# Scans of a gated DeltaNet block: side work queued behind the chain by edges, convolutions as a list of steps, the next head's preparation in 22 parts

## The chip, the cores and the metric

The kernel runs on one NeuronCore of a Trainium2 chip. A core has five engines with a queue each, which run side by side and wait for one another at semaphores: TensorE (PE; its weight loads are listed as PEld), VectorE (DVE), ScalarE (ACT), GpSimd (POOL) and SyncE (SP), which issues the DMAs here. The metric is the device time of one execution in microseconds; the time before is the median of three runs.

## The reference

One layer of a backbone over 512 latent tokens and 256 context tokens, width 2048, float32. A modulated RMS norm gives h (latents) and hc (context); one input projection feeds two groups of heads, and one output projection joins them.

```python
h = rms_norm(x, norm_w[l]) * (1.0 + scale) + shift
hc = rms_norm(ctx, norm_w[l]) * (1.0 + scale_c) + shift_c
...
qkv = jax.nn.silu(centred_conv(qkv, conv_w)).astype(jnp.float32)
...
def step(s, inp):
    q_i, k_i, u_i, w_i, g_i, intra_i = inp
    v_new = u_i - jnp.einsum('bhcd,bhde->bhce', w_i, s)
    o_i = (jnp.einsum('bhcd,bhde->bhce', q_i * jnp.exp(g_i)[..., None], s)
           + jnp.einsum('bhij,bhje->bhie', intra_i, v_new))
    g_last = g_i[..., -1:]
    s = (s * jnp.exp(g_last)[..., None]
         + jnp.einsum('bhcd,bhce->bhde', k_i * jnp.exp(g_last - g_i)[..., None], v_new))
    return s, o_i
```

Group A (8 heads of 128) is a gated delta rule in chunks of 64 tokens, one scan forward and one backward, over context and then latents, with a depthwise convolution of 5 taps and a SiLU on q, k and v ahead of it. Every chunk needs the inverse of a triangular 64x64 matrix. Group B (8 query heads, 2 key heads) is attention with per-head norms and rotary positions. Both are multiplied by SiLU gates.

## The kernel before, in words

All large matmuls are done in three passes of split numbers: a weight piece (512 rows by 128 columns, 256 KB) is loaded into wraw, cast on ScalarE into whi (L129), and VectorE subtracts to give wlo (L130); each has three buffers. `proj_steps` (L154) makes the 48 matmuls of a projection tile against h (512 columns, tile names kl, ql, vl, kvl, qal, zal) and, for k, v and the attention's keys and values, the same against hc (256 columns, kx, vx, kvx), from four pieces, and yields the columns of each step. It asks for a piece at the piece's first matmul.

Stages: an opening with modulation and the projections of head 0; a stretch of gates and preparation of head 0; eight scans, one a head; attention; the output projection and the final norm. The order on TensorE is the program's, by hand, up to the end of attention. On the other engines a planner orders the instructions at build time by priority (program order, moved up by `tc.high_priority`) and by when it reckons them ready; in attention ScalarE, VectorE and GpSimd are by hand too.

`gdn_scan` (L824) runs both directions of a head at once, in 12 steps. A step is a chain over engines: the state times the keys on TensorE (ks, L852 to L857), r on VectorE (L866, two halves), the triangular inverse UU times r on TensorE (ts, L875), two scaled copies vs (L879) and vn (L882) on ScalarE, the update on TensorE (L886), the new state st on VectorE (L892; L890 in a head's first step). Off the chain, GpSimd scales the old state into sd (L864, listed at L240), needed by st; ScalarE copies the state's part of the output from ks into oq (L871); TensorE adds the output of the chunk (L895). After ks, ts and the update the generator yields F1, F2 or F3 columns: 35 slots a head. In each slot the main loop (from L1169) does three things: `pull(n)` takes so many columns of the feed; if the slot is in PREP_AT, one part of the next head's preparation is done; in slot 6 the previous head's output is written.

The feed (`feeding`, L1098) is one long list of projection tiles: keys and values of attention, q0, v of head 1, then k, q and v of heads 2 to 7, with attention's tiles between and behind. At the end of a tile `take` (L195) copies it from PSUM into one of three buffers craw, and `gdn_post_k`, `gdn_post_q` or `gdn_post_v` queue at once a whole convolution (`conv`, L204): a scaled copy on ScalarE (L217), four taps on VectorE for the latents and four for the context (L221), a tanh on ScalarE (L224, L225), and two or four SiLU products on VectorE (L237).

`gdn_prep` (L621) makes a head's preparation in 11 parts, at slots 0, 2, 4, 6, 8, 15, 18, 27, 29, 31 and 33 of the scan before: transposed keys with sums of squares (t1 L640, t2 L646, t3 L653; copies and squares on ScalarE), the decay matrix gr (L681 to L686), the products of keys and queries (L693 to L713), transposes NT (L718), a transfer through DRAM (L728, L731), a substitution of 14 rounds on VectorE (tm, NE, L738 and L740), a transfer back (L744, L758), values (L751), and four stages of small matmuls (L771 to L813) up to UU (L821).

Of the kernel before, what the change touches and what calls it, by code (L numbers as in the profile page):

```python
# [68 lines left out]
def build(tc, a):  # L69
# [80 lines left out]
    def proj_tile(col, nm, pl, pc=None):  # L150
        for _ in proj_steps(col, nm, pl, pc):
            pass

    def proj_steps(col, nm, pl, pc=None):  # L154


        for kq in range(4):
            src = w_in[kq * 512:(kq + 1) * 512, col:col + 128].rearrange("(k p) c -> p k c", p=128)
            hi, lo = wpiece(src, f"{nm}_{kq}", 128, V)
            passes = [(kq * 4 + k4, n, lw, rt) for k4 in range(4)  # L160
                      for n, (lw, rt) in enumerate(hpass(kq * 4 + k4, hi[:, k4], lo[:, k4]))]

            def one(out, m, k, n, lw, rt):
                T.matmul(out, lhsT=lw, rhs=rt[m], start=k == 0 and n == 0, stop=k == KT - 1 and n == 2,  # L164
                         skip_group_check=True)

            if pc is not None and kq == 0:
                for out, m, n_ in ((pl, 0, SEQ), (pc, 1, CTX)):
                    for x in passes:
                        one(out, m, *x)  # L170
                        yield n_
                continue
            for x in passes:
                one(pl, 0, *x)
                if pc is not None:
                    one(pc, 1, *x)
                yield SEQ if pc is None else SEQ + CTX
# [17 lines left out]
    def take(pl, pc, raw=None, eng=None):  # L195

        raw = next_craw() if raw is None else raw
# [6 lines left out]
    def conv(t, nm, raw, ctx):  # L204
# [5 lines left out]
        acc = cvp.tile([128, 770], F32, tag="cacc", bufs=CA_BUFS, name=f"cacc_{nm}")  # L210
        acc = acc[:, :n]
# [4 lines left out]
        e = raw[:, 2:]  # L216
        S.activation(acc, raw[:, 0:n], AF.Copy, scale=w(0))  # L217
        for i0, m in ((off, SEQ), (0, CTX))[:2 if ctx else 1]:
            for j in range(1, 5):
                x = acc[:, i0:i0 + m]  # L220
                V.scalar_tensor_tensor(out=x, in0=raw[:, i0 + j:i0 + j + m], scalar=w(j), in1=x,  # L221
                                       op0=ALU.mult, op1=ALU.add)
        if ctx:
            S.activation(e[:, :CTX], acc[:, :CTX], AF.Tanh)  # L224
        S.activation(e[:, off:off + SEQ], acc[:, off:], AF.Tanh)  # L225
        return acc, e, off
# [349 lines left out]
    def next_craw():  # L576

        ncraw[0] += 1
        return craw[ncraw[0] % 3]
# [12 lines left out]

    def gdn_post_k(h, raw):
        kq = kq_of(h)
        kc = kcs[h] = qkp.tile([128, 2, 2, 64], F32, tag="kc", bufs=2, name=f"kc{h}")
        acc, e, off = conv(8 + h, f"k{h}", raw, True)
        x, y = [t[:, off:off + SEQ].rearrange("p (c t) -> p c t", t=64) for t in (acc, e)]
        silu(V, kq[:, 0:4, 0:64], x[:, 0:4], y[:, 0:4])
        silu(V, kq[:, 4:8, 64:128], x[:, 4:8], y[:, 4:8])
        x, y = [t[:, 0:CTX].rearrange("p (c t) -> p c t", t=64) for t in (acc, e)]  # L600
        silu(V, kc[:, :, 0], x[:, 0:2], y[:, 0:2])
        silu(V, kc[:, :, 1], x[:, 2:4][:, ::-1], y[:, 2:4][:, ::-1])

    def gdn_post_q(h, raw):
        kq = kq_of(h)
        acc, e, off = conv(h, f"q{h}", raw, False)
        x, y = [t[:, :SEQ].rearrange("p (c t) -> p c t", t=64) for t in (acc, e)]
        silu(V, kq[:, 0:4, 64:128], x[:, 0:4], y[:, 0:4])
        silu(V, kq[:, 4:8, 0:64], x[:, 4:8], y[:, 4:8])

    def gdn_post_v(h, raw):
        vv = vvs[h] = qkp.tile([128, 6, 2, 64], F32, tag="vv", bufs=1, name=f"vv{h}")
        acc, e, off = conv(16 + h, f"v{h}", raw, True)
        for p0_, n, o in ((2, 4, off), (0, 2, 0)):
            x, y = [t[:, o:o + n * 128].rearrange("p (c t) -> p c t", t=64) for t in (acc, e)]
            silu(V, vv[:, p0_:p0_ + n, 0], x[:, 0:n], y[:, 0:n])
            silu(V, vv[:, p0_:p0_ + n, 1], x[:, n:2 * n][:, ::-1], y[:, n:2 * n][:, ::-1])
# [3 lines left out]
    def gdn_prep(h):  # L621
# [3 lines left out]
        kq, kc, vv = kqs[h], kcs[h], vvs[h]  # L625
# [24 lines left out]
        yield  # L650
        t3 = gtile([128, 2, 128], f"t3{nm}")
# [4 lines left out]
        for p in range(2):  # L656
            S.activation(jk, t3[:, p], AF.Square, accum_out=ss[:, 8 + p:9 + p])

# [21 lines left out]

        V.tensor_tensor(out=gr, in0=gr, in1=gsc["gcum"][:, col].unsqueeze(2).to_broadcast([128, 12, 64]),  # L681
                        op=ALU.subtract)
        for v in range(2):
            V.tensor_tensor(out=gr[:, v * 6:v * 6 + 6], in0=gr[:, v * 6:v * 6 + 6],
                            in1=masks[v].unsqueeze(1).to_broadcast([128, 6, 64]), op=ALU.min)
        S.activation(gr, gr, AF.Exp)  # L686

# [13 lines left out]
        AT = gr  # L701
        V.tensor_tensor(out=gr, in0=gr, in1=cc[:, 1].unsqueeze(2).to_broadcast([128, 12, 64]), op=ALU.mult)
        for v in range(2):
# [10 lines left out]
        for half in range(2):  # L714
            vb = 1 - half
            for blk in range(2):
                b = half * 64 + blk * 32
                V.transpose(out=NT[b:b + 32, :, blk * 32:blk * 32 + 32],  # L718
                            in_=AT[b:b + 32, vb * 6:vb * 6 + 6, blk * 32:blk * 32 + 32])
# [12 lines left out]
        V.memset(NE.rearrange("w j i -> w (j i)")[:, 0:256:17], 1.0)  # L732
        tm = gp.tile([96, 64], F32, tag="tm", bufs=1, name=f"tm{nm}")
        with tc.high_priority(offset=1500):
            for m in range(14, 0, -1):
                n = 15 - m
                tv = tm[:, :m * n].rearrange("w (j i) -> w j i", i=n)
                V.tensor_tensor(out=tv, in0=NE[:, 0:m, m:m + 1].to_broadcast([96, m, n]),  # L738
                                in1=NE[:, m:m + 1, m + 1:].to_broadcast([96, m, n]), op=ALU.mult)
                V.tensor_tensor(out=NE[:, 0:m, m + 1:], in0=NE[:, 0:m, m + 1:], in1=tv, op=ALU.add)  # L740
        nd2 = nd2s[h % 2]
        for s in range(2):
            ds_ = slice(16 * s, 16 * s + 16)
            SY.dma_start(nd2[:, ds_, ds_], NE[48 * s:48 * s + 48])  # L744

        vtok = gp.tile([128, 6, 128], F32, tag="vtok", bufs=2, name=f"vtok{nm}")
        for p0_, n in ((0, 2), (2, 4)):
            yield
            tv_ = (btile if n == 2 else gtile)([128, n, 128], f"tv{nm}_{p0_}")
            for p in range(n):  # L750
                T.transpose(out=tv_[:, p], in_=vv[:, p0_ + p].rearrange("c s t -> c (s t)"), identity=ident)  # L751
            for p in range(n):
                S.activation(vtok[:, p0_ + p], tv_[:, p], AF.Copy, scale=vin[:, p0_ + p:p0_ + p + 1])

        DD = gp.tile([128, 12, 32], F32, tag="DD", bufs=1, name=f"DD{nm}")
        DT = gp.tile([128, 12, 32], F32, tag="DT", bufs=1, name=f"DT{nm}")
        for bi in range(4):
            SY.dma_start(DD[bi * 32:bi * 32 + 32], nd2[bi * 12:bi * 12 + 12].rearrange("w j i -> j w i"))  # L758

# [63 lines left out]

    def gdn_scan(h):  # L824
# [11 lines left out]
        for si, (v, p) in enumerate(steps):  # L836
# [10 lines left out]
            else:  # L847
# [11 lines left out]
                with first_of_all():  # L859
# [5 lines left out]
                    for rows, d in halves:  # L865
                        V.scalar_tensor_tensor(out=r[rows], in0=ks[rows, d], scalar=gsc["negeg"][rows, gcol:gcol + 1],  # L866
                                               in1=vtok[rows, p], op0=ALU.mult, op1=ALU.add)
                if lat:
                    with tc.high_priority(offset=1000):
                        for (rows, _), d in zip(halves, (db, dt_)):  # L870
                            S.activation(oq[rows, v, p - 2], ks[rows, d], AF.Copy,  # L871
                                         scale=gsc["egsw"][rows, gcol:gcol + 1])
# [3 lines left out]
            with first_of_all():  # L876
                if not last:
                    vs = gp2.tile([128, 128], F32, tag="vs", bufs=1, name=f"vs{nm}_{si}")
                    S.activation(vs, ts[:, 2], AF.Copy, scale=cc[:, 2, w:w + 1])  # L879
                if lat:  # L880
                    vn = gp2.tile([128, 128], F32, tag="vn", bufs=1, name=f"vn{nm}_{si}")
                    S.activation(vn, ts[:, 2], AF.Copy, scale=cc[:, 0, w:w + 1])  # L882
            yield F2
            if not last:
# [3 lines left out]
                with first_of_all():  # L888
                    if si == 0:
                        V.tensor_copy(sn, ts[:, 0:2])  # L890
                    else:
                        V.tensor_tensor(out=sn, in0=sd, in1=ts[:, 0:2], op=ALU.add)  # L892
# [134 lines left out]
    PREP_AT = (0, 2, 4, 6, 8, 15, 18, 27, 29, 31, 33)  # L1027
# [12 lines left out]
    gdn_post_v(0, raws[2])  # L1040
    gp = es_g.enter_context(tc.tile_pool(name="gp", bufs=1, reuse_waits="tile"))
# [14 lines left out]
    def feed_k(h):  # L1056
# [3 lines left out]
        gdn_post_k(h, take(pl, pc))  # L1060

    def feed_q(h):
        pl = PP.tile([128, SEQ], F32, tag="pl", name=f"ql{h}")
        yield from proj_steps(COL_Q + h * 128, f"q{h}", pl)
        gdn_post_q(h, take(pl, None))

    def feed_v(h):
# [3 lines left out]
        gdn_post_v(h, take(pl, pc))  # L1071
# [77 lines left out]
    for n in (3000, 5500, 5500, 4000, 14000):  # L1149
        pull(n)  # L1150
        next(prep, None)
    gdn_post_k(1, raws[3])
    pull(9000)
# [4 lines left out]
    gdn_post_q(1, raws[4])  # L1158
    es_x.close()
# [7 lines left out]
    run(prep, 5000, 24000, 5000, 7000, 6000)  # L1167
    tail = None
    for h in range(NH):  # L1169
# [3 lines left out]
        if h + 1 < NH:  # L1173
            prep, prep_at = gdn_prep(h + 1), PREP_AT
        else:
# [4 lines left out]
            prep, prep_at = attn_prep(), (*range(1, 28, 2), 33)  # L1180
        slot = 0
        for n in scan:
            if n is None:
                break
            pull(n)
            if slot in prep_at:
                next(prep, None)
            if slot == 6 and tail is not None:
                next(tail, None)
            slot += 1  # L1190
        for _ in prep:
# [427 lines left out]
```

## Time and profile before

| | us |
|---|---|
| time, median of 3 runs (1294.81 to 1297.11) | 1296.88 |
| the profiled execution | 1292.93 |
| its span, first to last instruction | 1291.1 |
| first scan's first ts to attention's first work, about 240 to 858 | 618 |
| attention, about 858 to 1103 | 245 |
| output projection and norm, 1103 to the end | 188 |

The profile lists busy time by engine, the time in stretches, waits by who waited for whom, and groups of instructions by line. A row of a timeline has the start in us from the span's start, the duration, engine and line, the operation, the tile written and the tiles read; a bracket gives the idle time before it and what ended it. A row of waits has the total in us, the number of waits and the longest. Ends of matmuls are modelled, so two matmuls in a row are drawn overlapping.

### The profile page before, as it was taken

How to read it: one execution, taken by the hardware profiler on the slowest of the kernel's cores; microseconds unless marked ns; L12 is line 12 of the kernel's file. 1: busy time of each engine (PE TensorE's matmuls, PEld its weight loads, DVE VectorE, ACT ScalarE, POOL GpSimd, SP SyncE). 2: the span in 40 equal slices, each digit the busy share in tenths (PEclk: the TensorE clock that was granted, in tenths of full speed). 3: DMA queues.
4: the chain of work that ended last, by engine and by line, in shares of the span. 5: the costliest groups of instructions: out<-in, count | busy, mean ns of one | idle time of the engine just before them, and what ended most of it. 6: DMA issues, size and time to landing. Idle time of an engine off the chain costs nothing. (4 is left out here: it accounts for less than half of the span.)

```text
span 1291.1 us, 24373 instructions
## 1 busy us (share of the span) xinstructions
PE 1241.8 (96%) x9242; PEld 1015.1 (79%) x9242; DVE 849.4 (66%) x1905; ACT 580.7 (45%) x1452; POOL 142.7 (11%) x206
## 2 busy tenths in 40 slices
PE   6899999999999999999999999999999999999997
PEld 4566688878788888888888787777888888788886
DVE  5444586686876769676786646546998997555333
ACT  5222363444545454454644444444455544434211
POOL 1323100111111111111211111100000000000000
PEclk9899999999999999999999999999999999999999
DMA  9999424232222312322232445347445353576302
GB/s 355 319 334 346 134 67 106 55 75 56 67 68 75 72 51 71 76 62 65 62 72 63 104 93 150 102 132 255 136 139 156 109 144 97 174 236 195 90 33 98
DMA packets 227288, 164.53 MB, mean 127 GB/s; under 512 B 62242, under 2 KB 198523, under 8 KB 226147
## 3 DMA queue, kind: packets, MB, share of 16 engines
q1 hardware_dynamic: 226874, 162.87, 43.5%
q8 instruction: 73, 1.20, 0.4%
q14 instruction: 44, 0.36, 0.1%
q10 hardware_dynamic: 297, 0.11, 0.0%
HBM read 148.85 MB, written 14.08 MB: 126 GB/s over the span
## 5 line engine op out<-in xcount | busy, mean ns | idle before, releaser
L240 POOL TENSOR_TENSOR sdh<-sth,egl 128x256 f32<-128x256 f32 x80 | 56.8, 711 | 447.9 <-DVE sth L892 345.3
L871 ACT ACTIVATE oqh<-ksh,egsw 64x128 f32<-64x128 f32 x128 | 46.4, 362 | 93.2 <-DVE rh L866 86.9
L866 DVE SCALAR_TENSOR_TENSOR rh<-ksh,negeg,vtokh 64x128 f32<-64x128 f32 x176 | 61.2, 348 | 31.0 <-PE ksh L854 24.4
L146 PE MATMUL po<-whi_wo,mh 128*128 128x512 f32 x192 | 76.2, 397 | 0.0
L148 PE MATMUL po<-whi_wo,ml 128*128 128x512 f32 x192 | 76.0, 396 | 0.0
L147 PE MATMUL po<-wlo_wo,mh 128*128 128x512 f32 x192 | 76.0, 396 | 0.0
L1358 PE MATMUL zl<-hhL,whi_z 128*128 128x512 f32 x176 | 71.4, 405 | 0.0
L1358 PE MATMUL zl<-hL,whi_z 128*128 128x512 f32 x176 | 69.8, 397 | 0.0
L1358 PE MATMUL zl<-hhL,wlo_z 128*128 128x512 f32 x176 | 69.3, 394 | 0.0
L130 DVE TENSOR_TENSOR wlo_wo<-wraw_wo,whi_wo 128x512 fp32r<-128x512 f32 x48 | 33.1, 690 | 51.5 <-ACT whi_wo L129 51.3
L886 PE MATMUL tsh<-vsh,ktok 128*128 128x128 f32 x352 | 56.6, 283 | 6.9 <-ACT vnh L882 3.5
L886 PEld LDWEIGHTS tsh<-vsh,ktok 128*128 128x128 f32 x352 | 47.3, 190 | 16.2 <-ACT vnh L882 8.1
L129 ACT CAST whi_wo<-wraw_wo 128x512 fp32r<-128x512 f32 x48 | 29.7, 620 | 62.3 <-PE po L148 52.1
L892 DVE TENSOR_TENSOR sth<-sdh,tsh 128x256 f32<-128x256 f32 x80 | 33.6, 420 | 27.4 <-PE tsh L886 19.2
L879 ACT ACTIVATE vsh<-tsh,cch 128x128 f32<-128x128 f32 x88 | 32.2, 366 | 38.8 <-PE tsh L875 37.5
L950 ACT CAST pth<-pt 128x512 fp32r<-128x512 f32 x48 | 26.5, 586 | 44.3 <-PE pt L1287 44.3
L164 PE MATMUL vl<-hhL,whi_v 128*128 128x512 f32 x112 | 46.3, 413 | 0.0
L164 PE MATMUL vl<-hhL,wlo_v 128*128 128x512 f32 x112 | 46.2, 413 | 0.0
L164 PE MATMUL vl<-hL,whi_v 128*128 128x512 f32 x112 | 45.8, 409 | 0.0
L1406 DVE SCALAR_TENSOR_TENSOR gacc<-graw,scol,gacc 128x512 f32<-128x512 f32 x60 | 44.9, 748 | 1.1
L146 PEld LDWEIGHTS po<-whi_wo,mh 128*128 128x128 f32 x192 | 36.1, 188 | 9.5 <-ACT ze L1312 0.8
L148 PEld LDWEIGHTS po<-whi_wo,ml 128*128 128x128 f32 x192 | 36.2, 188 | 8.8
(545 smaller groups left out, 3894.5 us busy)
## 6 DMA issues: line engine op xcount, KB each, us to landing
wada<-in_w_ada SPq DMA_DIRECT2D x64, 512.0 KB, 8.4
graw<-in_w_ada SPq DMA_DIRECT2D x64, 256.0 KB, 3.2
wraw_wo<-in_w_out SPq DMA_DIRECT2D x48, 256.0 KB, 3.1
wraw_z<-in_w_in SPq DMA_DIRECT2D x44, 256.0 KB, 3.0
wraw_v<-in_w_in SPq DMA_DIRECT2D x28, 256.0 KB, 2.9
wraw_k<-in_w_in SPq DMA_DIRECT2D x24, 256.0 KB, 2.8
wraw_q<-in_w_in SPq DMA_DIRECT2D x24, 256.0 KB, 2.8
xs<-in_x SPq DMA_DIRECT2D x4, 1024.0 KB, 5.2
```

The costliest lines, as they stand in the source:

```text
L130: (lo_eng or G).tensor_tensor(out=lo, in0=raw, in1=hi, op=ALU.subtract)
L146: T.matmul(out, lhsT=lh, rhs=rh, start=start, stop=False, skip_group_check=True)
L147: T.matmul(out, lhsT=lh, rhs=rl, start=False, stop=False, skip_group_check=True)
L148: T.matmul(out, lhsT=ll, rhs=rh, start=False, stop=stop, skip_group_check=True)
L164: T.matmul(out, lhsT=lw, rhs=rt[m], start=k == 0 and n == 0, stop=k == KT - 1 and n == 2, skip_group_check=True)
L240: eng.tensor_tensor(out=out, in0=x, in1=y, op=ALU.mult)
L866: V.scalar_tensor_tensor(out=r[rows], in0=ks[rows, d], scalar=gsc["negeg"][rows, gcol:gcol + 1], in1=vtok[rows, p], op0=ALU.mult, op1=ALU.add)
L871: S.activation(oq[rows, v, p - 2], ks[rows, d], AF.Copy, scale=gsc["egsw"][rows, gcol:gcol + 1])
L886: T.matmul(ts[:, d], lhsT=ktok[:, p, half], rhs=vs, start=True, stop=True, skip_group_check=True)
L892: V.tensor_tensor(out=sn, in0=sd, in1=ts[:, 0:2], op=ALU.add)
L1358: T.matmul(pl, lhsT=lw, rhs=rt, start=k == 0 and m == 0, stop=k == KT - 1 and m == 2, skip_group_check=True)
L1406: V.scalar_tensor_tensor(out=acc, in0=raw, scalar=scol[:, k:k + 1], in1=acc, op0=ALU.mult, op1=ALU.add)
```

## The change

Five things, all about order.

1. The scan keeps its latest chain instruction on VectorE (r, st) and on ScalarE (vs, vn) in `behind`. What a slot queues is traced inside `tc.issue_after` of these: each of its instructions on VectorE or ScalarE gets an edge that keeps it behind the chain's.
2. The copies oq go from ahead of ts to behind vn, with such an edge.
3. A convolution becomes a list of steps in a queue, `jobs`, each with its engine ("A" or "D") and a price. `step_jobs` does some of them at the end of a slot: steps of one kind only, VectorE's as long as the slot's budget CAP (1.0, 1.6 or 1.9 us) less what pieces and preparation spent of it lasts, ScalarE's not in the slots after ks. `finish` does all that must be done by then.
4. The preparation has 22 parts, with a price for each in PREP_AT; the rounds of the substitution, queued in slot 8 before, stand in five parts in slots 16 to 21.
5. A piece is loaded 4608 columns of matmuls ahead of its use, by a list (`plan`), instead of at its first matmul.

The instructions are the same in kind and number, and the feed has the same order.

```diff
+    def load_ahead():
+
+        if not plan:
+            return
+        col, nm, kq = plan.popleft()
+        src = w_in[kq * 512:(kq + 1) * 512, col:col + 128].rearrange("(k p) c -> p k c", p=128)
+        made[col, kq] = wpiece(src, f"{nm}_{kq}", 128, V)
+        spent[0] += 0.7
...
+            for ms, n_ in work:
+                if left > AHEAD >= left - n_:
+                    load_ahead()
+                left -= n_
+                for out, m, x in ms:
+                    one(out, m, *x)
+                yield n_
...
+        jobs.append(("A", 0, tag, first))
         for i0, m in ((off, SEQ), (0, CTX))[:2 if ctx else 1]:
             for j in range(1, 5):
...
+                jobs.append(("D", 0.75 if m == SEQ else 0.48, tag, lambda i0=i0, m=m, j=j: tap(i0, m, j)))
+        jobs.append(("A", 0, tag, tanh))
+        for f in last(accs, e, off):
+            jobs.append(("D", 0.42, tag, f))
+
+    def step_jobs(budget, act):
+
+        kind = None
+        while jobs and (kind is None or kind == jobs[0][0]) and (budget > 0 if jobs[0][0] == "D" else act):
+            kind, cost, _, fn = jobs.popleft()
+            fn()
+            budget -= cost
...
-                if lat:
-                    with tc.high_priority(offset=1000):
-                        for (rows, _), d in zip(halves, (db, dt_)):
-                            S.activation(oq[rows, v, p - 2], ks[rows, d], AF.Copy,
-                                         scale=gsc["egsw"][rows, gcol:gcol + 1])
...
+            if lat:
+                with tc.high_priority(offset=1000), tc.issue_after(behind["ACT"].ins):
+                    for (rows, _), d in zip(halves, (db, dt_)):
+                        S.activation(oq[rows, v, p - 2], ks[rows, d], AF.Copy,
+                                     scale=gsc["egsw"][rows, gcol:gcol + 1])
             yield F2
...
-    PREP_AT = (0, 2, 4, 6, 8, 15, 18, 27, 29, 31, 33)
+    PREP_AT = {0: 0, 3: 0, 4: 1.0, 5: 1.1, 6: 0, 7: 1.6, 8: 1.7, 9: 1.0, 10: 0.9, 11: 2.1, 15: 0, 16: 1.3, 17: 1.3,
+               18: 0, 19: 1.3, 20: 1.3, 21: 0.9, 26: 0.6, 27: 0.6, 29: 1.2, 31: 0.3, 33: 1.5}
+    LATE_AT = dict.fromkeys((*range(1, 28, 2), 33), 1.5)
+    CAP = (1.0, 1.6, 1.9)
...
-            pull(n)
-            if slot in prep_at:
-                next(prep, None)
-            if slot == 6 and tail is not None:
-                next(tail, None)
+            spent[0] = prep_at.get(slot, 0)
+            with ExitStack() as order:
+                for x in behind.values():
+                    order.enter_context(tc.issue_after(x.ins))
+                pull(n)
+                if slot in prep_at:
+                    next(prep, None)
+                if slot == 6 and tail is not None:
+                    next(tail, None)
+                step_jobs(CAP[slot % 3] - spent[0], slot % 3 < 2)
             slot += 1
```

More of the change, by code (lines that the diff above doesn't have):

```diff
@@ L1 @@
+from collections import deque
 from contextlib import ExitStack
@@ L165, in one @@
                          skip_group_check=True)
+            left = 12 * (SEQ if pc is None else SEQ + CTX)
             if pc is not None and kq == 0:
[L168 to L177, printed above, removed]
+                work = [(((out, m, x),), n_) for out, m, n_ in ((pl, 0, SEQ), (pc, 1, CTX)) for x in passes]
+            elif pc is not None:
+                work = [(((pl, 0, x), (pc, 1, x)), SEQ + CTX) for x in passes]
+            else:
+                work = [(((pl, 0, x),), SEQ) for x in passes]
+            for ms, n_ in work:
+                if left > AHEAD >= left - n_:
+                    load_ahead()
+                left -= n_
+                for out, m, x in ms:
+                    one(out, m, *x)
+                yield n_
     es_g = ExitStack()
@@ L202, in take, with conv @@
         return raw
-    def conv(t, nm, raw, ctx):
+    jobs = deque()
+    def conv(t, nm, tag, raw, ctx, last):
         n = SEQ + (CTX + 2 if ctx else 0)
@@ L209, in conv, with first, tap, tanh @@
             raw = raw[:, CTX + 2:]
-        acc = cvp.tile([128, 770], F32, tag="cacc", bufs=CA_BUFS, name=f"cacc_{nm}")
-        acc = acc[:, :n]
+        e = raw[:, 2:]
+        accs = []
         def w(j):
             return cvT[:, j * 24 + t:j * 24 + t + 1]
-        e = raw[:, 2:]
-        S.activation(acc, raw[:, 0:n], AF.Copy, scale=w(0))
+        def first():
+            accs.append(cvp.tile([128, 770], F32, tag="cacc", bufs=CA_BUFS, name=f"cacc_{nm}")[:, :n])
+            S.activation(accs[0], raw[:, 0:n], AF.Copy, scale=w(0))
+        def tap(i0, m, j):
+            x = accs[0][:, i0:i0 + m]
+            V.scalar_tensor_tensor(out=x, in0=raw[:, i0 + j:i0 + j + m], scalar=w(j), in1=x,
+                                   op0=ALU.mult, op1=ALU.add)
+        def tanh():
+            if ctx:
+                S.activation(e[:, :CTX], accs[0][:, :CTX], AF.Tanh)
+            S.activation(e[:, off:off + SEQ], accs[0][:, off:], AF.Tanh)
+        jobs.append(("A", 0, tag, first))
         for i0, m in ((off, SEQ), (0, CTX))[:2 if ctx else 1]:
             for j in range(1, 5):
[L220 to L226, printed above, removed]
+                jobs.append(("D", 0.75 if m == SEQ else 0.48, tag, lambda i0=i0, m=m, j=j: tap(i0, m, j)))
[8 more added lines that the diff above has]
+            budget -= cost
+    def finish(tag=None):
+        while jobs and (tag is None or any(x[2] == tag for x in jobs)):
+            jobs.popleft()[3]()
     def zero(t):
@@ L574, in build, with next_craw @@
     ncraw = [0]
-    def next_craw():
+    users = {}
+    def next_craw(tag=None):
         ncraw[0] += 1
-        return craw[ncraw[0] % 3]
+        k = ncraw[0] % len(craw)
+        if users.get(k) is not None:
+            finish(users[k])
+        users[k] = tag
+        return craw[k]
     qkp = es_g.enter_context(tc.tile_pool(name="qkp", bufs=1, reuse_waits="tile"))
@@ L595, in gdn_post_k, with last, part @@
         kc = kcs[h] = qkp.tile([128, 2, 2, 64], F32, tag="kc", bufs=2, name=f"kc{h}")
[L596 to L602, printed above, removed]
+        def last(accs, e, off):
+            def part(out, o, n, c0, c1, flip=False):
+                x, y = [t[:, c0:c1] for t in chunks(accs, e, o, n)]
+                silu(V, out, x[:, ::-1] if flip else x, y[:, ::-1] if flip else y)
+            return [lambda: part(kq[:, 0:4, 0:64], off, 8, 0, 4), lambda: part(kq[:, 4:8, 64:128], off, 8, 4, 8),
+                    lambda: part(kc[:, :, 0], 0, 4, 0, 2), lambda: part(kc[:, :, 1], 0, 4, 2, 4, True)]
@@ L604, in gdn_post_q, with last, part @@
+        conv(8 + h, f"k{h}", ("k", h), raw, True, last)
     def gdn_post_q(h, raw):
         kq = kq_of(h)
[L606 to L609, printed above, removed]
-    def gdn_post_v(h, raw):
[L612 to L617, printed above, removed]
+        def last(accs, e, off):
+            def part(out, c0, c1):
+                x, y = [t[:, c0:c1] for t in chunks(accs, e, 0, 8)]
+                silu(V, out, x, y)
+            return [lambda: part(kq[:, 0:4, 64:128], 0, 4), lambda: part(kq[:, 4:8, 0:64], 4, 8)]
@@ new lines, in gdn_post_q, with last, part @@
+        conv(h, f"q{h}", ("q", h), raw, False, last)
+    def gdn_post_v(h, raw):
+        def last(accs, e, off):
+            def part(p0_, n, o, flip):
+                if h not in vvs:
+                    vvs[h] = qkp.tile([128, 6, 2, 64], F32, tag="vv", bufs=1, name=f"vv{h}")
+                x, y = [t[:, n:2 * n][:, ::-1] if flip else t[:, 0:n] for t in chunks(accs, e, o, 2 * n)]
+                silu(V, vvs[h][:, p0_:p0_ + n, int(flip)], x, y)
+            return [lambda a=a, f=f: part(*a, f) for a in ((2, 4, off), (0, 2, 0)) for f in (False, True)]
+        conv(16 + h, f"v{h}", ("v", h), raw, True, last)
@@ L650, in gdn_prep @@
         yield
+        V.tensor_tensor(out=gr, in0=gr, in1=gsc["gcum"][:, col].unsqueeze(2).to_broadcast([128, 12, 64]),
+                        op=ALU.subtract)
+        yield
+        for v in range(2):
+            V.tensor_tensor(out=gr[:, v * 6:v * 6 + 6], in0=gr[:, v * 6:v * 6 + 6],
+                            in1=masks[v].unsqueeze(1).to_broadcast([128, 6, 64]), op=ALU.min)
+        yield
+        S.activation(gr, gr, AF.Exp)
         t3 = gtile([128, 2, 128], f"t3{nm}")
@@ L1152, in build @@
     gdn_post_k(1, raws[3])
+    finish()
     pull(9000)
@@ L1158, in build @@
     gdn_post_q(1, raws[4])
+    finish()
     es_x.close()
@@ L1193, in build @@
         tail = scan
+    finish()
     pull(12000)
```

115 lines of the change are left out of this document (70 added, 45 removed).

## The prediction

> **What bounds the kernel now.** I read the page first, then the busy time by stage (0 to 160 us opening, 160 to 240 first preparation, 240 to 858 the eight scans, then attention, then the output projection).
>
> ```profile
> span 1291.1 us, 24373 instructions
> PE 1241.8 (96%) x9242; PEld 1015.1 (79%) x9242; DVE 849.4 (66%) x1905; ACT 580.7 (45%) x1452; POOL 142.7 (11%) x206
> ...
> PE   6899999999999999999999999999999999999997
> ...
> PEclk9899999999999999999999999999999999999999
> ```
> ```profile
> core 0: us, PE busy (x) PEld busy (x) DVE busy (x) ACT busy (x) POOL busy (x), PEclk, DMA share, GB/s
> 160.00:240.00 80.00, 76.69 (x698) 64.43 (x698) 55.55 (x168) 38.34 (x91) 3.06 (x5) 0.96 0.35 86
> 240.00:858.00 618.00, 603.69 (x5464) 506.72 (x5463) 430.26 (x1082) 311.52 (x886) 88.84 (x128) 1.00 0.31 76
> ```
>
> TensorE runs the whole kernel in an order fixed by hand, and it is busy everywhere; its clock is full in the scans (1.00). No matmul is added or removed by the change, so it can gain only where TensorE waits: 618 - 603.69 = 14.3 us in the scans, 3.3 us before them. Attention and output come after the edited code and stay. Which waits these are, in the scans, for TensorE and then for its weight loads:
>
> ```profile
> PE tsh L875 <- DVE rh L866: 3.8, 7, 0.9
> PE tsh L886 <- ACT vnh L882: 3.5, 6, 1.1
> PE tsh L886 <- ACT vsh L879: 3.1, 5, 0.8
> PE tsh L875 <- DVE UU L821: 2.2, 4, 0.9
> PE ksh L857 <- DVE sth L890: 1.2, 1, 1.2
> PE ksh L852 <- DVE sth L892: 0.2, 1, 0.2
> PE ksh L857 <- DVE sth L892: 0.2, 1, 0.2
> ```
> ```profile
> PEld tsh L886 <- ACT vnh L882: 8.1, 15, 1.4
> PEld tsh L886 <- ACT vsh L879: 5.4, 7, 1.2
> PEld tsh L875 <- issue: 4.0, 12, 0.9
> PEld tsh L875 <- PE vx L164: 2.9, 5, 0.9
> PEld tsh L875 <- PE ql L164: 2.7, 5, 0.8
> ...
> PEld ksh L852 <- DVE sth L892: 2.2, 6, 0.6
> ...
> PEld vl L164 <- DVE wlo_v L130: 0.8, 2, 0.4
> ```
>
> All of the first list is the recurrence of the scan: state times keys (ks), r on VectorE, ts, vs and vn on ScalarE, the state update, st on VectorE. Between the links TensorE does slices of the next projections as cover (F1, F2, F3). A link waits when its VectorE or ScalarE step comes later than the cover ends. One such place, ScalarE and VectorE first, then TensorE:
>
> ```profile
> 284.11 0.71 DVE L866 SCALAR_TENSOR_TENSOR rh<-ksh,negeg,vtokh 64x128 f32<-64x128 f32 x2
> 284.85 0.75 DVE L221 SCALAR_TENSOR_TENSOR cacc_q<-craw,cvT,cacc_q 128x512 f32<-128x512 f32 x1
> 284.91 0.74 ACT L871 ACTIVATE oqh<-ksh,egsw 64x128 f32<-64x128 f32 x2 [2.91 <-DVE rh L866]
> 285.68 0.62 ACT L129 CAST whi_v<-wraw_v 128x512 fp32r<-128x512 f32 x1
> 286.20 0.63 ACT L225 ACTIVATE craw<-cacc_q 128x512 f32<-128x512 f32 x1
> 286.33 0.69 DVE L130 TENSOR_TENSOR wlo_v<-wraw_v,whi_v 128x512 fp32r<-128x512 f32 x1 [0.73 <-ACT whi_v L129]
> 286.85 0.37 ACT L879 ACTIVATE vsh<-tsh,cch 128x128 f32<-128x128 f32 x1
> ...
> 287.12 0.36 ACT L882 ACTIVATE vnh<-tsh,cch 128x128 f32<-128x128 f32 x1
> ...
> 288.38 0.42 DVE L892 TENSOR_TENSOR sth<-sdh,tsh 128x256 f32<-128x256 f32 x1 [0.69 <-PE tsh L886]
> ```
> ```profile
> 284.96 0.46 PE L875 MATMUL tsh<-rh,UU 128*128 128x128 f32 x2
> ...
> 285.97 0.39 PE L164 MATMUL vl<-hhL,whi_v 128*128 128x512 f32 x1
> 286.20 0.28 PE L164 MATMUL vx<-hhC,whi_v 128*128 128x256 f32 x1
> 287.53 0.71 PE L886 MATMUL tsh<-vsh,ktok 128*128 128x128 f32 x4 [1.05 <-ACT vnh L882]
> ```
>
> ts is done at 285.42 (284.96 + 0.46). ScalarE is then in oq, and after it does a weight cast and a tanh, so vs begins 1.43 us after its input is there, and TensorE stands for 1.05 us. This is queue order, not work: ScalarE is busy 311.52 of 618 us, VectorE 430.26. The pitch of cover is read off the starts: 285.97 to 286.20 is 0.23 us for 512 columns, 0.45 ns a column. F1 (3900 columns) covers 1.75 us, F2 (2700) 1.21, F3 (3200) 1.44.
>
> **The change part by part.** The profiled execution took 1292.93 us (span 1291.1 plus 1.8 outside it); the median of the runs is 1296.88, 4.0 above it. I make the sum against 1292.93 and carry the difference to the median. A change under 0.2% (2.6 us) can't be told from none.
>
> What there is to win: the first list adds up to 14.2 us in 25 waits. Each hides a little more, since a 256-column matmul is drawn 0.28 us long but its 256 columns take 0.12: 25 x 0.16 = 4.0, so 18.2 us. The 2.2 us on UU (with 4 x 0.16, 2.8) are at a head's first link, where the 22 parts end in the same slot 33 as the 11 did, with nothing between: these stay. Left are 15.4 us. The ends of this term: nothing (another instruction takes the blocker's place each time), and 25 us if the idle time of the weight loads at these links counted whole (8.1 + 5.4 + 4.0 + 2.9 + 2.7 + 2.2); I stay near TensorE's own rows, since in the place shown the next load may stand while a matmul still runs.
>
> *Edges (issue_after).* Everything that a slot queues on VectorE or ScalarE (weight pieces, preparation, convolution jobs) comes behind the chain's latest step there. It costs no instruction. An instruction under way is still not interrupted. On ScalarE, vs and vn are 0.37 + 0.36 us, both before L886 as the row shows; F2's 1.21 us leave 0.48 for a late start, so a cast of 0.62 just begun costs about 0.2. On VectorE a tap of 0.75 before st costs nothing while F3 (1.44) covers 0.75 + 0.42. For such remainders I put 3.4 us back, some 40 to 45 joints at 0.08; their ends are 0 and the 15.4 itself.
>
> *oq.* The two copies (0.74 us) go from ahead of vs to behind vn. Same work; in the rows above it saves vs up to 0.2 us (ts done 285.42, oq ends 285.65) in 64 latent steps. It is part of the 15.4, not added. Who waits for it later is the sum at the end of a head and the ks bank two steps on: no cost.
>
> *Convolutions as jobs.* Per head 30 VectorE and 6 ScalarE jobs, exactly the instructions of before, so nothing added; k of head 4, say, is ready in slot 8 of scan 2, q in 16, v in 27 (counted from the columns of the slots). The VectorE budget of a scan is 1.0 + 1.6 + 11 x 4.5 = 52.1 us; preparation is priced 19.7, some 13 pieces 9.1, jobs 17.0: 45.8. With the chain (12 x 1.13 = 13.6 us from the rows 0.71 and 0.42) VectorE has 59 us of work in 77. By this count the queue is empty or down to a few jobs at each head's end, and finish() forces nothing inside a scan: 0 us; if 6 us of taps were forced at a head's start, its first link would stand 6 less the cover of F2 and F3 (2.65), 23 in all for seven heads. Head 1's v convolution moves out of the stretch before the scans, where TensorE doesn't wait for it, into scan 0: 0.
>
> *Preparation in 22 parts.* t2's copy and squares move from slot 2 (an F1, ahead of vs) to 3, and t3's from 4 to 6; the decay ops get slots of their own; the triangular inverse goes from slot 8 on, as early as possible, to slots 16 to 21, its transfers issued in 11 and 21:
>
> ```profile
> DMA to landing us min/median/max: 2.2/2.6/2.7
> ```
>
> A slot is 77/35 = 2.2 us, so five slots (11 us) lie ahead of each reader, for a write and a read back of 2.6 us each (the row is for the tile of the inverse, NE). SP's queue has weight loads between; they may hold it for a few us and still fit. 0 us, with a VectorE stall of a few us a head if they don't.
>
> *Pieces loaded ahead.* A piece is now requested 4608 columns (2.07 us) before its use, and its subtraction waits behind r or st. It needs 0.62 + 0.69 = 1.31 us, so 0.76 are left. Until now three buffers set the lead, and TensorE's loads waited 0.8 us in all for pieces. I put 0: pieces come before preparation and jobs within a slot. Its upper end is the second rival below.
>
> *Shared work of VectorE and GpSimd.* st also frees sd on GpSimd, and from now on two-input VectorE work follows st in most steps, beside sd:
>
> ```profile
> 359.64 0.21 DVE L740 TENSOR_TENSOR NEh<-NEh,tmh 96x56 f32<-96x56 f32 x1
> 359.88 0.42 DVE L892 TENSOR_TENSOR sth<-sdh,tsh 128x256 f32<-128x256 f32 x1
> 360.21 0.21 DVE L738 TENSOR_TENSOR tmh<-NEh 96x56 f32<-96x56 f32 x1
> 360.38 0.62 POOL L240 TENSOR_TENSOR sdh<-sth,egl 128x256 f32<-128x256 f32 x1 [6.11 <-DVE sth L892]
> 360.45 0.61 DVE L740 TENSOR_TENSOR NEh<-NEh,tmh 96x56 f32<-96x56 f32 x1
> ```
>
> The op that takes 0.21 us in the first row takes 0.61 in the last and ends at 361.06, just behind sd's 361.00: 0.4 us lost to VectorE. st 0.42 + budget 1.6 + 0.4 = 2.42 us from the update; ks is done at 1.44 + 0.46 (two matmuls, as those of ts), so r starts 0.5 late, ends 0.5 + 0.7 = 1.2 after ks, and F1 covers 1.75. I take 0. The Trainium skill (SBUF — State Buffer, section "SBUF: two separate sides") says that a GpSimd op and a VectorE op with two SBUF inputs exclude each other for a whole instruction, and the later one blocks. By that rule each of the 80 sd can hold a piece of the new side work, 32 us of VectorE time in all; were none of it absorbed, the sum would be a loss of 20 us, not a gain of 12. The trace agrees with the rule in the rows above; how much is absorbed they can't show.
>
> Sum: 15.4 - 3.4 = 12 us. 1292.9 - 12 = 1280.9 for a profiled execution like this one, 1296.9 - 12 = 1284.9 for the median: **1285 us**, with its own range of 1281 to 1291 (nearly all of the 15.4 gone, or four tenths of it).
>
> **The rivals.** *All loss at the links goes* (chance 0.11): loads and short waits below the list go too, some 20 us of the 25, 1277. For it: 13.5 us of load waits at L886 alone. Against it: an instruction under way still holds up a link.
>
> *No change* (0.14), 1297: another cast or tap is always under way when a link comes, or a part that is now behind a chain step makes TensorE wait at a preparation matmul. For it: vs and vn alone fill two thirds of F2. Against it: the place above shows two whole foreign instructions between ts and vs, which the edges forbid.
>
> *Slower by late pieces* (0.12): the edges take the lead from weight pieces. The place is L164 waiting for wlo; the k, q and v of heads 2 to 7 are 72 pieces; with 0.76 us left and one tap (0.75) ahead the margin is nil, and with a late st on top a piece is 0.3 us late: 72 x 0.3 = 21.6, 12 is regained, 1296.9 + 9.6 = 1306.5. It decides from 12/72 = 0.17 us a piece. For it: the subtraction is last in a row of three. Against it: the budgets leave VectorE 18 us a head.
>
> *Slower by sd beside side work* (0.08): with the 0.4 us at sd and one op more than the budget says (0.75) in front of r, r ends 0.2 after F1 (1.2 + 0.75 - 1.75). In all 80 steps that is 16 us, less the 12: 1301. It decides from 0.15 us a step. For it: st and sd meet in every step. Against it: r itself reads one operand from PSUM and doesn't meet sd.
>
> **How the numbers follow.** The forecast has 0.55. Faster by over 0.2%: 0.55 + 0.11 + 0.04 of the no-change case = 0.70. Within 0.2%: 0.08. Slower: 0.02 + 0.12 + 0.08 = 0.22. The range runs from 1275, just past the largest gain, to 1300; left out are most of the two slower cases.
>
> **What would show it.** Right: L886's waits on vs and vn under 2 us in all; vs within 0.3 us of ts; oq after vn; the stretch of the scans about 606 us; busy times of all engines as before; the waits on UU unchanged. Wrong: L164 waiting for wlo over 5 us (late pieces); r's wait at L875 over 4 us with sd beside VectorE work longer than 0.62 (the lock); waits at L693 to L813 (preparation); the chain's waits gone with the stage no shorter, which would mean that the drawn waits weren't TensorE's loss.

## The result, and the profile after

The changed kernel takes 1281.18 us (median of 4 runs, 1280.09 to 1282.18), the kernel before, now with a fourth run, 1295.85 us on the same chip (1294.02 to 1297.11). The ratio is 0.989, 95% interval 0.9875 to 0.9904: 12 to 16 us gained. The profiled execution took 1281.33 us, 11.6 less than that of before; its span is 11.9 shorter.

The page's first lines, and busy time by stage with the scans' stage cut where they begin and end now (after the length: busy us and number of PE, PEld, DVE, ACT and POOL, then clock, DMA share and GB/s):

```profile
span 1279.2 us, 24270 instructions
...
PE 1237.9 (97%) x9242; PEld 1019.8 (80%) x9242; DVE 851.9 (67%) x1905; ACT 568.7 (44%) x1452; POOL 151.6 (12%) x206
```
```profile
160.00:241.00 81.00, 76.99 (x696) 64.99 (x697) 54.55 (x166) 36.31 (x88) 2.69 (x5) 0.96 0.32 81
241.00:846.00 605.00, 597.27 (x5463) 509.07 (x5463) 433.93 (x1084) 302.14 (x888) 98.06 (x127) 1.00 0.32 78
846.00:1091.00 245.00, 241.69 (x1349) 203.46 (x1351) 199.18 (x325) 118.13 (x260) 10.32 (x9) 1.00 0.50 150
1091.00:1279.00 188.00, 180.09 (x824) 147.05 (x816) 86.30 (x145) 61.34 (x118) 2.21 (x4) 0.99 0.42 139
```

All of it lies in the scans, 618 to 605 us; the stretch before them is 1 us longer, attention and output the same. The work is the same too: TensorE 5464 and 5463 matmuls in the trace, VectorE 430 and 434 us. ScalarE's drawn time fell from 312 to 302 us, though its largest groups take as long as before (oq 46.4 and 45.8 us, vs 32.2 and 32.3). TensorE's idle time in the stage fell from 14.3 to 7.7 us and its drawn busy time from 603.7 to 597.3: half of the gain was never drawn as idle time. Its waits in the scans, and then those of its weight loads at the links ("issue" is time in which the engine waited for nothing that the profile shows):

```profile
PE tsh L956 <- DVE rh L951: 6.0, 8, 2.5
PE tsh L956 <- DVE UU L904: 1.3, 2, 0.9
PE vtp L1041 <- DMA kvch<-kvd: 0.6, 1, 0.6
PE tsh L972 <- ACT vsh L960: 0.5, 2, 0.3
```
```profile
PEld tsh L956 <- issue: 8.1, 18, 2.9
PEld tsh L956 <- PE vx L185: 3.9, 7, 0.9
...
PEld tsh L972 <- ACT vsh L960: 1.0, 2, 0.5
```

The update (L972, L886 before) has stopped waiting: 6.6 us to 0.5, its loads 13.5 to 1.0. The new state's waits at ks are gone (1.6 us). What waits more than before is ts for r: 3.8 to 6.0. A plain reading of the queue is who ended ScalarE's idle time ahead of vs, here from the view of its line, before and then after (us, times):

```profile
  PE tsh L875: 37.5, 27
```
```profile
  PE tsh L956: 215.7, 75
```

Before, in 27 of the 88 steps ScalarE stood ready when ts came, and in the others it was at other work. Now it stands ready in 75. The count shows the order and not the gain: it is 71 in the run with 11 parts below, which gained nothing, and 61 in the fastest version.

### The profile page after: what moved, and what is told of

The parts are those of the page before. It is cut to its first block, busy times and chain, and to the rows that moved or that the text cites. A ratio compares the mean times of both kernels' runs of the same rounds, so it can differ in the third digit from the quotient of the medians.

```text
span 1279.2 us, 24270 instructions
## 1 busy us (share of the span) xinstructions
PE 1237.9 (97%) x9242; PEld 1019.8 (80%) x9242; DVE 851.9 (67%) x1905; ACT 568.7 (44%) x1452; POOL 151.6 (12%) x206
## 4 chain that ended last, share of the span: by engine, by line
PE 79%; DVE 10%; DMA 4%; ACT 3%; issue 3%; SPq 0%; POOL 0%; ACTq 0%; POOLq 0%; DVEq 0%
PE zl L1459 9%; PE kl L185 4%; PE po L147 4%; PE po L149 4%; PE po L148 4%; PE vl L185 4%; PE ql L185 4%; PE kvl L185 3%; PE tsh L972 3%; PE ada L404 2%; PE kx L185 2%; PE vx L185 2%; PE tsh L956 2%; PE klat L471 2%; PE pt L1388 2%
## 5 line engine op out<-in xcount | busy, mean ns | idle before, releaser
L960 ACT ACTIVATE vsh<-tsh,cch 128x128 f32<-128x128 f32 x88 | 32.3, 367 | 215.7 <-PE tsh L956 215.7
L289 POOL TENSOR_TENSOR sdh<-sth,egl 128x256 f32<-128x256 f32 x80 | 67.3, 841 | 451.8 <-DVE sth L978 353.4
L972 PE MATMUL tsh<-vsh,ktok 128*128 128x128 f32 x352 | 54.4, 277 | 0.5 <-ACT vsh L960 0.5
L972 PEld LDWEIGHTS tsh<-vsh,ktok 128*128 128x128 f32 x352 | 48.1, 191 | 4.1 <-ACT vsh L960 1.0
L967 ACT ACTIVATE oqh<-ksh,egsw 64x128 f32<-64x128 f32 x128 | 45.8, 357 | 0.8
L956 PE MATMUL tsh<-rh,UU 128*128 128x128 f32 x176 | 37.7, 296 | 6.3 <-DVE rh L951 6.0
```

The costliest lines, as they stand in the source:

```text
L289: eng.tensor_tensor(out=out, in0=x, in1=y, op=ALU.mult)
L956: T.matmul(ts[:, 2], lhsT=UU[:, w], rhs=r, start=True, stop=True, skip_group_check=True)
L967: S.activation(oq[rows, v, p - 2], ks[rows, d], AF.Copy, scale=gsc["egsw"][rows, gcol:gcol + 1])
L972: T.matmul(ts[:, d], lhsT=ktok[:, p, half], rhs=vs, start=True, stop=True, skip_group_check=True)
```

## The experiments

Times are medians; ratios are to the kernel before on the same chip, with 95% intervals, and the changed kernel's own is 0.989. Two theories went in: that the edges carry the gain and the rest is neutral, and, as rival A, that spreading the side work carries it and the edges are not needed.

**Without the edges.**

```diff
-                for x in behind.values():
-                    order.enter_context(tc.issue_after(x.ins))
```

> The changed kernel without the edges on what a slot queues (oq keeps its edge behind vn). Theory, that the gain of about 14.7 us comes from the edges, which keep side work behind the chain's steps: most of the gain goes, time 1290 to 1298, L972 (the update) waits again for vs and vn, over 4 us in all. Rival A, that budgets, job list and 22 parts do it by themselves because no slot has too much side work: time within 3 us of the changed kernel's 1281, waits at the update under 2 us.

1295.76 us, ratio 1.001 (0.9998 to 1.0022). All of the gain goes. TensorE's longest waits in the scans of that run:

```profile
PE tsh L956 <- DVE rh L951: 6.3, 12, 0.8
PE tsh L956 <- DVE UU L904: 3.9, 4, 2.1
PE ksh L942 <- DVE sth L976: 2.3, 1, 2.3
PE ksh L937 <- DVE sth L978: 1.8, 3, 1.3
PE tsh L972 <- ACT vsh L960: 0.5, 2, 0.3
PE tsh L972 <- ACT vnh L963: 0.5, 2, 0.2
```

Rival A falls: parts, budgets and lead alone give nothing. But the theory's picture was wrong too. The update waits 1.0 us here (its loads 3.4), so ScalarE's links come nearly right without edges; which of the other edits does that wasn't tried. What comes back is at VectorE's links: r, UU and st take 14.3 us in the first four rows, against 7.6 before. Against the changed kernel r hardly differs, 6.3 and 6.0; UU goes from 1.3 to 3.9 and st from 0 to 4.3. The longest of these, 2.3 us for st and 2.1 for UU, stand behind VectorE instructions that were themselves waiting for a transfer: 3.32 us for a rotary table and 2.22 for the decay row that gr is made from.

**The edges alone**, on the kernel before, with r, st, vs and vn recorded in `behind` as in the changed one:

```diff
-            pull(n)
-            if slot in prep_at:
-                next(prep, None)
-            if slot == 6 and tail is not None:
-                next(tail, None)
+            with ExitStack() as order:
+                for x in behind.values():
+                    order.enter_context(tc.issue_after(x.ins))
+                pull(n)
+                if slot in prep_at:
+                    next(prep, None)
+                if slot == 6 and tail is not None:
+                    next(tail, None)
```

> The kernel before with the edges alone: whole convolutions queued at once, 11 parts, oq ahead of vs, pieces at their first matmul. Theory (edges carry the gain): faster than before by 7 us or more, 1283 to 1289. Rival A (the distribution carries it, edges alone only change which work is late): within 4 us of before's 1296, with waits of matmuls of the preparation (L640 to L813) or for weight pieces (wlo) that before didn't have.

1438.22 us, ratio 1.1107 (1.1086 to 1.1127): 144 us slower than before. So the first theory falls as well. The scans' stage and the longest of TensorE's waits:

```profile
241.00:1003.00 762.00, 651.67 (x5465) 528.16 (x5466) 432.53 (x1085) 307.46 (x889) 101.28 (x127) 0.95 0.25 62
```
```profile
PE ql L164 <- DVE wlo_q L130: 31.9, 17, 6.4
PE kl L164 <- DVE wlo_k L130: 14.0, 10, 2.7
PE kl L164 <- ACT whi_k L129: 11.9, 8, 3.5
```

No chain link is among the nine largest rows of these waits: all are weight pieces. The links did come right: over the stage r, UU, st and vs make 4.0 us of waits, the update 0.2 of it, though a TensorE that stands elsewhere also gives them more time. The edges hold casts and subtractions behind the chain, and the feed, which shares TensorE's queue with the chain, stands for them. This is the prediction's rival of late pieces, at full size.

**Pieces without a lead**, in the changed kernel: a piece is asked for at the last matmul of the one before.

```diff
-    AHEAD = 4608
+    AHEAD = 0
```

> The changed kernel with each weight piece asked for at the last matmul of the piece before it instead of 4608 columns ahead. If the lead matters with edges (the rival of late pieces in the prediction, worked from 0.76 us of margin): waits of L185 for wlo of 0.5 us or more a piece, 1300 or slower. If the planner pulls the pieces up anyway, as far as the three buffers let it: within 3 us of 1281 and no such waits.

1372.17 us, ratio 1.06 (1.0579 to 1.0621), 92 us behind the changed kernel.

```profile
PE kvl L185 <- ACT whi_kv L130: 7.8, 4, 3.2
PE ql L185 <- ACT whi_q L130: 7.5, 8, 1.6
PE kl L185 <- DVE wlo_k L131: 5.9, 7, 1.4
```

**Half the lead**, 1.04 us:

```diff
-    AHEAD = 4608
+    AHEAD = 2304
```

> The changed kernel with pieces asked for 2304 columns (1.04 us) ahead instead of 4608 (2.07 us); without a lead it was 1372. By the prediction's margin (cast 0.62 and subtraction 0.69 make 1.31 us, so 0.76 are left at 4608): the cast and subtraction no longer fit, each piece is 0.3 us late or more, 1300 to 1330 and waits of L185 for wlo and whi. If the planner pulls the pieces up by itself and only the very last position hurts: within 5 us of the changed kernel.

1289.22 us, ratio 0.9967 (0.9955 to 0.9979); the changed kernel beside it 0.9899.

```profile
PE tsh L956 <- DVE rh L951: 5.2, 8, 1.7
PE ql L185 <- ACT whi_q L130: 2.2, 2, 1.2
```

9 us are lost, less than expected. Nine waits for pieces make 6.9 us: 1.04 us of lead is too short for some pieces, not for each; why so few was not tried (a cast that finds ScalarE free before the slot's chain step would do it). The full lead has no such wait at all. The three leads give 1372, 1289 and 1280: without any lead the edges are ruinous, and the second half of it is worth 9 us.

**Convolutions at once**, behind the edges (the same line also after q and v):

```diff
         gdn_post_k(h, take(pl, pc, tag=("k", h)))
+        finish()
```

> The changed kernel with each convolution queued whole at the end of its projection, behind that slot's chain steps, instead of in budgeted steps. Theory (edges carry the gain, the list only spreads work that VectorE has room for): up to 6.6 us of taps stand behind one chain step; VectorE's next step r or st waits unless the planner puts it ahead; loss 0 to 5 us. Rival A (distribution carries it): loss 8 us or more, r and st late by whole taps.

1328.66 us, ratio 1.0259 (1.0238 to 1.028), 48 us behind: a loss of the size that rival A gave, at a place that neither expectation named.

```profile
PE ql L185 <- DVE wlo_q L131: 16.5, 6, 3.2
PE pxah L854 <- DVE DTh L846: 12.2, 5, 4.0
PE tsh L956 <- DVE rh L951: 4.1, 5, 2.1
```

r doesn't wait for whole convolutions (4.1 us, less than in the changed kernel); the planner still brings it ahead. The taps and products, 6.6 us for k or v, delay what is queued behind them: the pieces of the next tile, and the transposes DTh that the preparation's matmuls need. At the two longest of the latter, 4.0 and 3.9 us, six taps in a row (3.26 us) and four products (1.16 us) stand ahead of DTh; at two shorter ones VectorE itself stood over 3 us for the cast of a piece of the next k.

**The preparation in 11 parts**, at the slots of before, all rounds of the substitution queued in slot 8:

```diff
-        if h == 0:
+        if True:
             parts = parts[1:3] + parts[4:] + [parts[0], parts[3]]
...
-    PREP_AT = {0: 0, 3: 0, 4: 1.0, 5: 1.1, 6: 0, 7: 1.6, 8: 1.7, 9: 1.0, 10: 0.9, 11: 2.1, 15: 0, 16: 1.3, 17: 1.3,
-               18: 0, 19: 1.3, 20: 1.3, 21: 0.9, 26: 0.6, 27: 0.6, 29: 1.2, 31: 0.3, 33: 1.5}
+    PREP_AT = {0: 0, 2: 0, 4: 3.7, 6: 3.6, 8: 8.2, 15: 0, 18: 0.6, 27: 0.6, 29: 1.2, 31: 0.3, 33: 1.5}
+    TIMES = {4: 4, 6: 3, 8: 6, 18: 2}
...
-                if slot in prep_at:
+                for _ in range(TIMES.get(slot, 1) if slot in prep_at and h + 1 < NH else slot in prep_at):
                     next(prep, None)
```

> The changed kernel with the preparation in the 11 parts and slots of before (t2 in slot 2, t3 and the decay in slot 4, all rounds of the substitution queued in slot 8); edges, jobs and oq stay as changed. Theory: t2's and t3's copies and squares come ahead of vs again in slots 2 and 4: loss 2 to 5 us, seen as waits of the update for vs in the first steps of a head. Rival A: loss 7 us or more. Rival B (the parts do nothing): within 2 us of 1281.

1294.68 us, ratio 1.0011 (0.9997 to 1.0025): 15 us, the whole gain.

```profile
PE tsh L956 <- DVE rh L951: 7.0, 13, 1.8
PE ql L185 <- DVE wlo_q L131: 4.2, 3, 1.8
PE tsh L972 <- ACT vsh L960: 1.9, 4, 1.0
```

The expected waits for vs are there and small, 1.9 us against 0.5, and r adds 1.0. Most of the new waits are for pieces, 5.3 us, which come at about slots 10 to 13 of a scan (2.2 us a slot), behind the lumps that slots 4 to 8 queue on VectorE.

**oq ahead of ts again**, where it stood before:

```diff
+                if lat:
+                    with tc.high_priority(offset=1000):
+                        for (rows, _), d in zip(halves, (db, dt_)):
+                            S.activation(oq[rows, v, p - 2], ks[rows, d], AF.Copy,
+                                         scale=gsc["egsw"][rows, gcol:gcol + 1])
                 yield F1
...
-            if lat:
-                with tc.high_priority(offset=1000), tc.issue_after(behind["ACT"].ins):
```

> The changed kernel with the two oq copies ahead of ts again, as before. Theory: oq between r and vs makes vs late by about 0.2 us in 64 steps, mostly within F2's spare 0.5 us; loss 1 to 4 us, and the update's waits for vs and vn come back in part (1 to 4 us). Rival: oq was half of the gain or more, since it stood right ahead of vs in every latent step: loss 7 us or more.

1276.35 us, ratio 0.9867 (0.9849 to 0.9885). No loss: at least equal, and rather 3 us faster, though the intervals overlap. The update waited 0.3 us for vs. In the changed kernel, moving oq is no part of the gain.

**Two waits of the changed kernel.** The longest of r's waits, 2.5 us, is in the last head's second step:

```profile
771.66 0.69 DVE L289 TENSOR_TENSOR IB<-IB,nw 128x512 f32<-128x512 f32 x1 [2.97 <-DMA IB<-in_rope]
...
772.97 0.71 DVE L951 SCALAR_TENSOR_TENSOR rh<-ksh,negeg,vtokh 64x128 f32<-64x128 f32 x2
...
773.82 0.55 PE L956 MATMUL tsh<-rh,UU 128*128 128x128 f32 x1 [2.51 <-DVE rh L951]
```

VectorE stood 2.97 us for the transfer of a rotary table (which lies in the buffer IB) with r queued behind it. Its products, and those of the second table, put some parts later (the place of the first is shown):

```diff
                 yield
+                if kv == 0 and t0 == 2:
+                    rope_scale(tabk, 1)
                 tp = transposes(chs, t0, n, bank(f"kps{kv}{t0}")[:, :n])
```

> The changed kernel with the two products that scale the rotary tables moved to a later part, so that VectorE doesn't stand for the table's transfer ahead of r in the last head's second step (r waited there 2.5 us on TensorE's side). Theory (a VectorE instruction whose input hasn't landed holds up the chain behind it, which neither edge nor budget prices): the wait of 2.5 us goes, 2 to 3 us faster than the changed kernel, 1278 to 1279. Rival: another instruction takes its place, no change.

1276.72 us, ratio 0.9868 (0.9854 to 0.9882), and that wait is gone:

```profile
PE tsh L956 <- DVE rh L951: 3.5, 7, 1.1
```

The other kind is sd beside side work, here in the changed kernel's first scan:

```profile
288.07 0.42 DVE L978 TENSOR_TENSOR sth<-sdh,tsh 128x256 f32<-128x256 f32 x1
288.41 0.68 DVE L131 TENSOR_TENSOR wlo_v<-wraw_v,whi_v 128x512 fp32r<-128x512 f32 x1
288.57 1.00 POOL L289 TENSOR_TENSOR sdh<-sth,egl 128x256 f32<-128x256 f32 x1 [5.55 <-DVE sth L978]
289.01 1.89 DVE L248 SCALAR_TENSOR_TENSOR cacc_q<-craw,cvT,cacc_q 128x512 f32<-128x512 f32 x2
290.83 0.71 DVE L951 SCALAR_TENSOR_TENSOR rh<-ksh,negeg,vtokh 64x128 f32<-64x128 f32 x2
291.65 0.30 PEld L956 LDWEIGHTS tsh<-rh,UU 128*128 128x128 f32 x2 [0.88 <-PE vx L185]
291.68 0.35 PE L956 MATMUL tsh<-rh,UU 128*128 128x128 f32 x1 [0.59 <-DVE rh L951]
```

sd takes 1.00 us here, and two taps take 1.89 where two free ones take 1.50: a budget of two taps becomes one of two and a half, and r is late. With sd on ScalarE:

```diff
-                        mul(G, sd, st, (eg if dt_ == 0 else eg[:, ::-1]).to_broadcast([128, 2, 128]))
+                        for d in range(2):
+                            S.activation(sd[:, d], st[:, d], AF.Copy, scale=eg[:, d if dt_ == 0 else 1 - d])
```

> The changed kernel with the scaled old state sd made on ScalarE (two copies with a scale, about 0.74 us a step) instead of on GpSimd (0.84 us mean). If the two-input taps are blocked by sd (1.11 us instead of 0.75 beside it): the longest tap falls to 0.75 us, VectorE's busy time in the scans falls by 10 to 30 us, r's waits at ts fall by 1 to 2 us. Against it stands ScalarE's 0.74 us in the F1 slots, in which vs of the same step may come late. Theory: lock absorbed, time within 3 us of 1281. Rival (the lock costs 0.15 us a step or more): 1270 or faster.

1275.89 us, ratio 0.9865 (0.9848 to 0.9882). The taps of q, with GpSimd beside them and then without (last figures: busy us, mean ns, idle before):

```profile
L248 DVE SCALAR_TENSOR_TENSOR cacc_q<-craw,cvT,cacc_q 128x512 f32<-128x512 f32 x24 | 19.6, 817 | 0.4
```
```profile
L248 DVE SCALAR_TENSOR_TENSOR cacc_q<-craw,cvT,cacc_q 128x512 f32<-128x512 f32 x24 | 17.9, 747 | 0.3
```

and the scans with sd on ScalarE, busy times by engine and then r's waits:

```profile
241.00:842.00 601.00, 595.49 (x5467) 509.18 (x5468) 419.23 (x1086) 351.02 (x1050) 31.45 (x48) 1.00 0.32 79
```
```profile
PE tsh L957 <- DVE rh L952: 3.3, 5, 1.8
```

VectorE's busy time falls from 433.93 to 419.23 us with the same instructions: 15 us were time in which two-input work stood for sd; the kernel gains about 3. Most of that stood there before the change as well, 430.26 us against 419.23. ScalarE takes 49 us more and has the room.

Each of these two is about 3 us, hardly more than the intervals allow to tell. So the changed kernel ran again beside combinations, on one chip.

> The changed kernel itself, unedited, beside the three others on the same chip, so that differences of 3 us can be told. Expected 0.989 of before (0.9875 to 0.9904), about 1280.

1280.03 us (1277.71 to 1283.17), ratio 0.9899 (0.9884 to 0.9914).

> The changed kernel with the rotary tables scaled later and sd on ScalarE, oq behind vn as changed. Theory (two separate waits of TensorE: 2.5 us for the table's transfer, 1 to 3 us for r beside sd): 4 to 6 us faster than the changed kernel, 1274 to 1277, r's waits at ts under 2 us. Against the version with oq ahead of ts it shows what the place of oq is worth when ScalarE also makes sd: 0 to 2 us either way.

Table and sd: 1274.38 us (1274.23 to 1275.15), ratio 0.9855 (0.9841 to 0.9868).

> The changed kernel with three edits that each came out about 3 us faster: oq ahead of ts again, the rotary tables scaled later, sd on ScalarE. If they act at different waits (oq on none, the table on one wait of 2.5 us in the last head, sd on r's waits beside sd): the gains add, 1271 to 1275. If oq and sd meet on ScalarE ahead of vs: waits of the update for vs over 2 us and no more than 1276 to 1279.

Table, sd and oq ahead of ts: 1271.75 us (1270.11 to 1273.56), ratio 0.9834 (0.982 to 0.9847). This is the fastest version, 8 us under the changed kernel beside it and clear of its interval. Its scans and all of TensorE's waits there:

```profile
241.00:841.00 600.00, 597.30 (x5518) 511.79 (x5505) 421.27 (x1088) 354.28 (x1055) 31.43 (x49) 1.00 0.33 79
```
```profile
PE tsh L962 <- DVE UU L904: 1.2, 2, 0.9
PE tsh L962 <- DVE rh L952: 1.2, 4, 0.6
PE tsh L973 <- ACT vsh L966: 0.2, 1, 0.2
```

2.6 us of waits are left of 14.2. That it beats the version with table and sd alone, by 2.6 us, is likely and not shown: the four times of each lie apart, the intervals overlap.

## Why the prediction was right, and where it was not

The time was forecast as 1285 with 1281 to 1291 counted out for the likeliest case; 1281.18 came, at its lower end. The gain was forecast as 12 us; it is 11.6 between the profiled executions and 14.7 between medians.

*What there is to win.* That the waits are queue order and not work is shown: with the same instructions they go from 14.2 to 8.4 us (and to 2.6 in the last version, where sd is on another engine). The size was right by two errors that cancelled, which is luck. Of the 15.4 us called removable the drawn waits gave back only 5.8; another 6.4 came out of TensorE's drawn busy time, of which 25 times 0.16 us had been allowed for, 4.0, tied to the waits listed. This points to more stands too short to be drawn: the loads' idle time at the links (ks, ts and the update) fell from 33 us over all its rows, of which the prediction quoted six with 25, to 16. No run separates such stands from the way matmuls are drawn. The upper end of 25 was nearer to the matter than it looked.

*Edges.* Right that they hold foreign work behind the chain, and wrong about where they are needed. The place shown was ScalarE's. There either half is nearly enough: the update waits 0.2 us with the edges alone and 1.0 without them, against 6.6 before, though without them ScalarE stands ready in only 58 of 88 steps. Beside the other edits the edges are worth the whole gain, and what they save of drawn waits is almost all at VectorE's st and UU.

*oq.* Wrong. It was counted into the 15.4; with it back ahead of ts nothing is lost, and beside the two other edits the time is 2.6 us lower, with overlapping intervals. In the place shown before, the cast and the tanh behind oq stood between it and vs; with these held back oq still fits in front. Why it is rather faster there is open: in the first of these runs no wait for r passes 1.0 us, the one behind the table included, so that some of it is another order by the planner.

*Convolutions as jobs, preparation in 22 parts, pieces ahead.* The forecast cost each at nothing, and each cost nothing: no wait for a piece, none for a preparation matmul but 0.6 us for a transfer in the last head. What it missed is that none is optional. Take one away and 15 to 92 us go, and 9 with half the lead, though all of them without the edges gain nothing. Of the rivals, late pieces were the true danger: at a lead of zero they cost 92 us, at half the lead 9. The margin of 0.76 us was the right kind of number, and it held: the changed kernel has no wait for a piece. As a price it is too high: half the lead makes it 0.27 us short, 19 us over 72 pieces, and 9 were lost.

*sd beside side work.* Right in mechanism, absorbed only in part: sd grew from 57 us (711 ns mean) to 67 (841), and r's waits, 6.0 us, passed the 4 us set as a sign, but 2.5 of them are the table's. With table and sd mended r's waits fall to 1.5 us, and the time by 5.7. The Trainium skill's rule (SBUF — State Buffer, section "SBUF: two separate sides", exclusive use of the shared ports by GpSimd or by two-input VectorE work) fits all of this: q's taps go from 817 to 747 ns when sd leaves GpSimd. Of the 32 us worked out as its worst case for the new side work about 4 came, 433.93 us less 430.26; the other 11 of the 15 were there before.

*UU* was said to stay; it fell from 2.2 to 1.3 us. *Before the scans* 0 was forecast and 1 us was lost: a matmul of the gates (L596) now waits 2.7 us for VectorE, while a wait of 2.1 us for a weight piece is gone. No run followed that.

## What to carry to other kernels

When a serial chain shares in-order queues with plenty of side work, look at each link for whether its engine stands ready when the input comes, and price what is queued in front of it. Edges that let the chain go first are only half of an edit: whatever they hold back must be cut into pieces that fit the gaps and asked for early enough, or its own readers stand instead. Instructions whose input comes by a transfer belong in no queue ahead of the chain until that input has landed.

## What the runs showed of the hardware

Waits of a few us cost more than their length here. In the scans the granted clock was 1.00 before and after; with the edges alone it was 0.95 over the stage, and the same matmuls were drawn busy for 651.67 us instead of 603.69, beside 110 us of idle time. There single waits reached 6.4 us; in the changed kernel none passes 2.5. By an estimate from these numbers the clock makes 32 of the 48 us (603.69 / 0.95 = 635); the rest is open. The length of the waits seems to count, not their sum: without a lead TensorE stood 66 us in the stage, no wait over 3.3, at 0.98; with whole convolutions at once 39 us, waits up to 4.0, at 0.97. The Trainium skill (TensorE: Matmul & The Clock Gate, Part 1) has the clock fall after an idle window of about 3.4 us; the runs agree in kind, and can't show the length.
